# Placing the first head's keys before its queries, spreading the top-k search, and subtracting low parts by accumulating DMAs

## The chip, the cores and the metric

The kernel runs on one core of a Trainium2 chip. The metric is device time in microseconds (us) of one execution. The engines are TensorE (PE for matmuls, PEld for its weight loads), VectorE (DVE), ScalarE (ACT), GpSimd (POOL) and SyncE (SP), whose queue issues most of the DMAs.

## The reference

One decoder layer on 512 tokens of width 1024: a half-step SwiGLU FFN, a mixer with two attention branches, and a second half-step FFN.

```python
x = x + 0.5 * swiglu_ffn(x, ffn1_norm, ...)
h = rms_norm(x, mix_norm)
(fq, fk, fv, ff, dq, dk, dv, iq, ik, iw, ga, gb) = split_columns(h @ w_in)
# branch A, 8 heads: forgetting attention
o_a = softmax(norm(fq) @ norm(fk).T * scale + cum[t] - cum[s], causal) @ fv     # cum = cumsum(log_sigmoid(ff + b))
# branch B, 8 heads with one shared key and value: only the 128 best keys of each query
score = sum_h iw[t, h] * relu(iq[t, h] . ik[s])
o_b = softmax(norm(dq) @ norm(dk).T * scale + bias[t - s], on top_k(score, 128)) @ dv
merged = sigmoid(ga) * (o_a @ w_branch_a) + sigmoid(gb) * (o_b @ w_branch_b)
x = x + merged @ w_out
x = x + 0.5 * swiglu_ffn(x, ffn2_norm, ...)
```

(The two softmax lines are shortened here; the reference works in blocks of 128 queries.)

## The kernel before

Every fp32 operand is split into a high part in TensorE's fast format and a low part, the rest, and a product is three matmuls (lines 130 to 132): high by high, low by high, high by low. For a weight, SP loads a chunk of 128 x 1024 into one of three raw buffers (`ra`, `rb`, `rc`), ACT casts it to the high part `wh` (line 124), and `lo_eng` subtracts to make the low part `wl` (line 125). `wh` and `wl` have three buffers each, so the cast of a chunk waits until TensorE has left the chunk three places earlier. In the mixer `lo_eng` is GpSimd until head 2 and VectorE after that.

The mixer's projections are "units", kept in one list: w_s (small columns), four units of indexer queries, then the 256-column units fk0, fq0, fv0, fk1, fq1, fv1, dq0, dq1 (keys, queries and values of four forgetting heads each, then queries of the sparse branch), then gates and branch products. A 256-column unit has two chunks of 48 matmuls each. `prod.run(us, upto)` issues TensorE work from this list for so many microseconds by a fixed table price (0.64 for six matmuls of 256 columns), not beyond unit `upto`. TensorE's order is written out by hand; the other engines' order comes from a scheduler, and each engine works strictly in its order.

When fk0 or fq0 is done, `normed` (ACT `kn` L627, ACT `sqh` L519, DVE `ss` L521 and L522, POOL `rh` L524, POOL `kn` L630) normalizes it. `get_k` and `get_q` transpose one head pair on TensorE (`ps_k`, `ps_q`, L530), split the result on ACT (`hi`) and DVE (`lo`, L514) and `place` the halves by DMAs on SP's queue (four for queries, eight for keys).

After the indexer products (`ps_ix`) comes a prelude to the 16 heads: TensorE works on fk0, fq0 and fv0 while VectorE runs the top-k search, 16 rounds of `max` and `match_replace` (L767, L769) over three score tiles, 99 steps in all. In that prelude also stand the keys of the sparse branch (`dsa_keys`: DVE scales `sd` by `rh`, L722, TensorE transposes it to `ps_dk`) and the forget gate's cumulative sum (`forget`: matmuls `pc`, DVE `cum`, transposes `ps_ct`). Then each head g has four steps s: weigh the head before (`pt` transposes, `po` products), one softmax block (`ps_qk`, DVE L817, ACT L819, POOL L821), and `prod.run(FILL[g], limit)`, which fills TensorE's time. `limit` is unit 13 (the last 256-column unit) for heads below 6, the four early gates up to head 9 step 1, and everything after.

The prelude before the change:

```python
while prod.at < 7:                      # through fk0 and fq0
    prod.run(MM); topk_run(TOPK_PRE)    # TOPK_PRE = 2 search steps
for g in later: next(g, 0)              # dsa_keys, forget: ps_dk, pc
for step in range(14):
    prod.run(MM, 8); topk_run(TOPK_PRE) # fv0
    # step 5: ps_ct, step 7: get_q(0), step 10: get_k(0), step 12: bias
prod.finish(8)
```

In the second half of the heads the bias of the mask (`b`) is made on POOL for every softmax block (L893 and L894, later L897).

Of the kernel before, what the change touches and what calls it, by code (L numbers as in the profile page):

```python
# [11 lines left out]
F32 = mybir.dt.float32  # L12
F32R = mybir.dt.float32r
AF = mybir.ActivationFunctionType
OP = mybir.AluOpType
# [3 lines left out]
P = 128  # L19
# [8 lines left out]
FILL = (2.1, 2.3, 2.0, 2.0, 1.7, 1.7, 1.7, 1.7, 2.0, 2.0, 1.4, 1.5, 1.2, 1.2, 1.9, 2.3)  # L28
FILL_LAST = 0.8
FILL_IX = 0.5  # L30
TOPK_PRE, TOPK_BEAT = 2, 1
EARLY_GATES = 4
MM = 0.64
WARM = 9
# [3 lines left out]
EPS = 1e-6  # L38
BIG = 1e30
S_W = 208  # L40
GA = ("g_ffn1", "g_mix", "g_ffn2")


# [7 lines left out]
def tile_hybrid_layer(ctx: ExitStack, tc: tile.TileContext, a: dict):  # L51
# [48 lines left out]
    lo_eng = [V]  # L100
# [5 lines left out]
    def raw_tile(tag):  # L106
        return wpool.tile([P, 1024], F32, tag=tag, bufs=1, name=tag)

    def split_w(raw, f=1024):
        wh = wpool.tile([P, 1024], F32R, tag="wh", name="wh")  # L110
        wl = wpool.tile([P, 1024], F32R, tag="wl", name="wl")
        S.copy(wh[:, :f], raw[:, :f])  # L112
        V.tensor_sub(wl[:, :f], raw[:, :f], wh[:, :f].bitcast(F32))  # L113
        return wh, wl

    def load_w(src, n, m, raw=None):
        f = n * m
        if raw is None:
            raw = raw_tile(next(raw_tags))
        wh = wpool.tile([P, 1024], F32R, tag="wh", name="wh")  # L120
        wl = wpool.tile([P, 1024], F32R, tag="wl", name="wl")
        with tc.high_priority(offset=1 if first else 30):
            nc.sync.dma_start(raw[:, :f].rearrange("p (n m) -> p n m", n=n), src)
            S.copy(wh[:, :f], raw[:, :f])
            lo_eng[0].tensor_sub(wl[:, :f], raw[:, :f], wh[:, :f].bitcast(F32))
        return (wh[:, :f].rearrange("p (n m) -> p n m", n=n),
                wl[:, :f].rearrange("p (n m) -> p n m", n=n))

# [365 lines left out]
    with tc.tile_pool(name="mix", bufs=1) as mp, ExitStack() as att_ctx:  # L494
# [79 lines left out]
        def tm_proj(ws, cols, done):  # L574

            def run():
                ps = [acc_tile("ps_t")[:, :2 * cols].rearrange("p (u c) -> p u c", u=2) for _ in range(2)]
                for c in range(2):
                    wh, wl = ws[c]()
                    for t in range(NT):  # L580
                        for kk in range(4):
                            k = 4 * c + kk
                            mm3(ps[t // 2][:, t % 2], xh[k][:, t * P:(t + 1) * P], xl[k][:, t * P:(t + 1) * P],
                                wh[:, kk], wl[:, kk], k == 0 and t % 2 == 0, k == KD - 1 and t % 2 == 1)
                            if (c, t, kk) != (1, 3, 3):
                                yield MM / 2
                done(ps)
                yield MM / 2
            return run

        chunks = []

        def weight(src, n, m):

            me = len(chunks)
            chunks.append([src, n, m, None])

            def take():
                for c in chunks[me:me + 3]:
                    if c[3] is None:  # L600
                        c[3] = load_w(*c[:3])
                return chunks[me][3]
            return take

        def small_done(ps):
# [53 lines left out]
            gb.append(g)  # L659

        def tm256(name, n, done):
            return tm_proj([weight(a[name][n][:, 4 * c:4 * c + 4], 4, 256) for c in range(2)], 256, done)

        oA = ([mp.tile([P, T], F32R, tag=f"oh{c}", name="oAh") for c in range(4)],
              [mp.tile([P, T], F32R, tag=f"ol{c}", name="oAl") for c in range(4)])
        units = [tm_proj([weight(a["w_s"][:, 4 * c:4 * c + 4], 4, S_W) for c in range(2)], S_W, small_done)]
        units += [fm_proj(weight(a["w_iq"][c], KD, P), (xh, xl), KD, iq_done) for c in range(4)]
        units += [tm256("w_fk", 0, normed("fk0")), tm256("w_fq", 0, normed("fq0")), tm256("w_fv", 0, values(0)),
                  tm256("w_fk", 1, normed("fk1")), tm256("w_fq", 1, normed("fq1")), tm256("w_fv", 1, values(1)),
# [109 lines left out]
        def topk_run(n):  # L779

            nonlocal topk_debt
            topk_debt += n
            with tc.issue_after(anchor[0].ins) if anchor[0] else nullcontext():
                while topk_debt >= 1:
                    next(topk, 0)
                    topk_debt -= 1
# [71 lines left out]
        def get_q(g):  # L858

            nm, c = ("fq", g // 2) if g < H else ("dq", g // 2 - 4)  # L860
            prod.finish({"fq0": 7, "fq1": 10, "dq0": 12, "dq1": 13}[f"{nm}{c // 2}"])
            gain = gq[:, 0:1] if g < H else gq[:, 1:2]
            parts = halves(columns(tn[f"{nm}{c // 2}"], c % 2, "ps_q"), gain)
            out = [at.tile([P, T], F32R, tag=tag, bufs=2, name="st") for tag in ("qh", "ql")]
            for hf, st in enumerate(out):
                place(st, hf, parts[0], hf)
                place(st, 1 - hf, parts[1], hf)
            return out
# [29 lines left out]
                return b[:, :n]  # L898
            return bias

        while prod.at < 7:
            prod.run(MM)
            topk_run(TOPK_PRE)
        for g in later:
            next(g, 0)
        for step in range(14):
            prod.run(MM, 8)
            topk_run(TOPK_PRE)
            if step == 5:
                next(later[1], 0)  # L910
            if step == 7:
                nq = get_q(0)
            if step == 10:
                nk = get_k(0)
            if step == 12:
                nb = get_bias(0)
        prod.finish(8)


        probs = {}  # L920
        flipped = None
# [172 lines left out]
```

## Time and profile before

| | |
|---|---|
| three runs, us | 1115.91, 1113.08, 3799.8 |
| median, us | 1115.91 |
| span of the profiled execution, us | 1111.9 |
| instructions | 17413 |
| busy in the span | PE 98%, PEld 87%, DVE 69%, ACT 49%, POOL 20% |

No device time stands beside the profiled execution's span; the two close runs are 1.2 and 4.0 us above it. A profile row gives the start, the duration, the engine, the line, the operation and its tiles; in square brackets stands how long the engine sat idle before it and what ended that. TensorE's matmuls overlap, so the spacing of their starts, not their duration, tells what one costs.

### The profile page before, as it was taken

The page shows a single profiled execution, that of the slowest core. Times are in us where ns is not written, and L with a number is a line of the kernel's source. Part 1 is how long each engine was busy: PE and PEld are TensorE (multiplying, and loading weights), DVE is VectorE, ACT ScalarE, POOL GpSimd, SP SyncE. Part 2 cuts the span into 40 slices and gives each one's busy share as a digit, 9 for nine tenths or more (in the row PEclk, how much of TensorE's full clock was granted, in tenths as well). Part 3 has the DMA queues.
Part 4 walks back from the last instruction along what each step waited for, and adds up shares of the span by engine and source line. Part 5 has one row for each costly group of instructions (what it writes and reads, how often), then busy time and mean ns, then how long its engine had stood idle before and what let it go on. Part 6 is the DMA issues. An engine that isn't in the chain of part 4 may idle for free.

```text
span 1111.9 us, 17413 instructions
## 1 busy us (share of the span) xinstructions
PE 1084.2 (98%) x6664; PEld 967.0 (87%) x6664; DVE 769.8 (69%) x1228; ACT 539.5 (49%) x862; POOL 218.5 (20%) x263
## 2 busy tenths in 40 slices
PE   8999999999999997899999999999999999999998
PEld 6788899989988897899778778888889899989997
DVE  5995578746966599966664666764976478755963
ACT  5653155513644653467655676443544245522551
POOL 0000000000002347677842561000000000000000
PEclk9999999999999999899999999999999999999999
DMA  7334235532442224335324411433245325432441
GB/s 244 107 98 146 88 97 151 139 100 84 110 115 92 76 76 118 110 112 151 101 76 143 122 59 38 126 121 97 93 124 143 94 77 153 135 97 91 124 115 67
DMA packets 43236, 122.61 MB, mean 110 GB/s; under 512 B 5641, under 2 KB 6025, under 8 KB 43153
## 3 DMA queue, kind: packets, MB, share of 16 engines
q1 hardware_dynamic: 38976, 113.89, 33.7%
q0 software_dynamic: 4032, 7.34, 3.9%
q8 instruction: 53, 0.87, 0.3%
q10 hardware_dynamic: 144, 0.26, 0.1%
q14 instruction: 31, 0.25, 0.1%
HBM read 103.63 MB, written 2.11 MB: 95 GB/s over the span
## 4 chain that ended last, share of the span: by engine, by line
PE 81%; DVE 8%; ACT 4%; POOL 3%; issue 3%; DMA 2%; SPq 0%; POOLq 0%; DVEq 0%; ACTq 0%
PE pd L131 7%; PE pd L132 7%; PE pd L130 7%; PE pB L132 4%; PE pB L131 4%; PE pB L130 4%; PE pC L132 3%; PE pA L132 3%; PE pA L131 3%; PE pC L131 3%; PE pA L130 3%; PE pC L130 3%; PE ps_f L130 2%; PE ps_f L131 2%; PE ps_f L132 2%
## 5 line engine op out<-in xcount | busy, mean ns | idle before, releaser
L131 PE MATMUL pd<-al,wh 128*128 128x512 f32 (+1 forms) x294 | 113.4, 386 | 0.5 <-DVE al L207 0.5
L130 PE MATMUL pd<-ah,wh 128*128 128x512 f32 (+1 forms) x294 | 113.4, 386 | 0.2
L132 PE MATMUL pd<-ah,wl 128*128 128x512 f32 (+1 forms) x294 | 113.1, 385 | 0.0
L205 POOL DMA_DIRECT2D al<-gu x20 | 17.1, 855 | 428.9 <-ACT al L204 428.9
L112 ACT CAST wh<-s 128x1024 fp32r<-128x1024 f32 x48 | 50.6, 1055 | 93.9 <-PE pB L131 39.3
L406 DVE SCALAR_TENSOR_TENSOR x<-pd,x 128x512 f32<-128x512 f32 (+1 forms) x49 | 33.3, 680 | 88.6 <-PE pd L132 88.4
L130 PE MATMUL ps_t<-wh,xh 128*128 128x256 f32 (+1 forms) x288 | 83.2, 289 | 0.0
L131 PE MATMUL ps_t<-wl,xh 128*128 128x256 f32 (+1 forms) x288 | 82.7, 287 | 0.0
L132 PE MATMUL ps_t<-wh,xl 128*128 128x256 f32 (+1 forms) x288 | 82.6, 287 | 0.0
L130 PE MATMUL pB<-tbh,wh 128*128 128x256 f32 x256 | 71.4, 279 | 0.0
L131 PE MATMUL pB<-tbl,wh 128*128 128x256 f32 x256 | 71.4, 279 | 0.0
L132 PE MATMUL pB<-tbh,wl 128*128 128x256 f32 x256 | 71.4, 279 | 0.0
L130 PEld LDWEIGHTS pd<-ah,wh 128*128 128x128 f32 x294 | 55.2, 188 | 11.9 <-ACT ah L202 1.0
L131 PEld LDWEIGHTS pd<-al,wh 128*128 128x128 f32 x294 | 55.2, 188 | 11.8 <-DVE al L207 1.1
L132 PEld LDWEIGHTS pd<-ah,wl 128*128 128x128 f32 x294 | 55.2, 188 | 11.0
L113 DVE TENSOR_TENSOR wl<-s,wh 128x1024 fp32r<-128x1024 f32 x48 | 58.5, 1219 | 3.8 <-ACT wh L112 3.8
L131 PEld LDWEIGHTS ps_t<-wl,xh 128*128 128x128 f32 x288 | 56.7, 197 | 0.5
L130 PEld LDWEIGHTS ps_t<-wh,xh 128*128 128x128 f32 x288 | 56.8, 197 | 0.4
L132 PEld LDWEIGHTS ps_t<-wh,xl 128*128 128x128 f32 x288 | 56.7, 197 | 0.0
L112 ACT CAST wh<-re 128x1024 fp32r<-128x1024 f32 (+1 forms) x27 | 27.8, 1028 | 57.4 <-PE pd L131 22.2
L112 ACT CAST wh<-ra 128x1024 fp32r<-128x1024 f32 (+1 forms) x29 | 29.8, 1029 | 51.6 <-PE pd L131 23.4
L819 ACT ACTIVATE p<-p,mn 128x512 f32<-128x512 f32 (+1 forms) x64 | 35.9, 561 | 37.0 <-DVE mn L817 36.8
(326 smaller groups left out, 3604.9 us busy)
## 6 DMA issues: line engine op xcount, KB each, us to landing
rc<-in_w_pair_dram SPq DMA_DIRECT2D x13, 512.0 KB, 3.6
re<-in_w_pair_dram SPq DMA_DIRECT2D x13, 512.0 KB, 3.6
ra<-in_w_pair_dram SPq DMA_DIRECT2D x13, 512.0 KB, 3.5
rd<-in_w_pair_dram SPq DMA_DIRECT2D x13, 512.0 KB, 3.6
rb<-in_w_pair_dram SPq DMA_DIRECT2D x12, 512.0 KB, 3.7
al<-gu POOLq DMA_DIRECT2D x20, 256.0 KB, 4.1
ra<-in_w_down_dram SPq DMA_DIRECT2D x7, 512.0 KB, 3.5
rc<-in_w_down_dram SPq DMA_DIRECT2D x7, 512.0 KB, 3.6
```

The lines of the kernel that those rows point to most:

```text
L112: S.copy(wh[:, :f], raw[:, :f])
L113: V.tensor_sub(wl[:, :f], raw[:, :f], wh[:, :f].bitcast(F32))
L130: PE.matmul(out, lh, rh, start=start, stop=False, **more)
L131: PE.matmul(out, lh, rl, start=False, stop=False, **more)
L132: PE.matmul(out, ll, rh, start=False, stop=stop, **more)
L205: G.dma_start(l, u, accum_op=OP.add)
L406: V.scalar_tensor_tensor(x[d][:, cols], ps, 0.5, x[d][:, cols], op0=OP.mult, op1=OP.add)
L819: S.activation(p, p, AF.Exp, bias=mn, scale=-1.0, accum_out=rs)
```

## The change

The prelude is now counted in table time: 53 steps of 0.64, until 33.5 is reached, with one search step each instead of two, up to unit 9, so that most of fk1 is done there too. At table times, "milestones" issue the rest: at 2.0 the sparse keys and the cumulative sum, at 7.0 the transposes of the sum, at 16.6 the keys of head 0, at 27.6 its queries, at 28.6 its bias. The chunks of all 256-column units get their low part from ACT (`wl = -wh`) and a DMA on GpSimd's queue that adds the raw chunk to it. The tiles `wh` and `wl` grow from 1024 to 1088 columns, and the chunks of the 256-column units and of w_s lie 8 columns (32 bytes) into theirs.

```diff
-TOPK_PRE, TOPK_BEAT = 2, 1
+TOPK_PRE, TOPK_BEAT = 1, 1
+PRELUDE = 33.5
+W_COLS, W_AT = 1088, 8
...
-    def load_w(src, n, m, raw=None):
+    def load_w(src, n, m, raw=None, at=0):
...
-        wh = wpool.tile([P, 1024], F32R, tag="wh", name="wh")
-        wl = wpool.tile([P, 1024], F32R, tag="wl", name="wl")
+        wh, wl = (wpool.tile([P, W_COLS], F32R, tag=nm, name=nm)[:, at:at + 1024] for nm in ("wh", "wl"))
         with tc.high_priority(offset=1 if first else 30):
             nc.sync.dma_start(raw[:, :f].rearrange("p (n m) -> p n m", n=n), src)
             S.copy(wh[:, :f], raw[:, :f])
-            lo_eng[0].tensor_sub(wl[:, :f], raw[:, :f], wh[:, :f].bitcast(F32))
+            if lo_eng[0] is None:
+                S.mul(wl[:, :f], wh[:, :f].bitcast(F32), -1.0)
+                G.dma_start(wl[:, :f], raw[:, :f], accum_op=OP.add)
+            else:
+                lo_eng[0].tensor_sub(wl[:, :f], raw[:, :f], wh[:, :f].bitcast(F32))
...
         def tm256(name, n, done):
-            return tm_proj([weight(a[name][n][:, 4 * c:4 * c + 4], 4, 256) for c in range(2)], 256, done)
+            return tm_proj([weight(a[name][n][:, 4 * c:4 * c + 4], 4, 256, W_AT, True) for c in range(2)], 256, done)
...
-        units = [tm_proj([weight(a["w_s"][:, 4 * c:4 * c + 4], 4, S_W) for c in range(2)], S_W, small_done)]
+        units = [tm_proj([weight(a["w_s"][:, 4 * c:4 * c + 4], 4, S_W, W_AT) for c in range(2)], S_W, small_done)]
...
-        while prod.at < 7:
-            prod.run(MM)
+        ahead = {}
+        milestones = [(2.0, lambda: [next(g, 0) for g in later]),
+                      (7.0, lambda: next(later[1], 0)),
+                      (16.6, lambda: ahead.update(k=get_k(0))),
+                      (27.6, lambda: ahead.update(q=get_q(0))),
+                      (28.6, lambda: ahead.update(b=get_bias(0)))]
+        spent = 0.0
+        while spent < PRELUDE:
+            prod.run(MM, 9)
+            spent += MM
             topk_run(TOPK_PRE)
-        for g in later:
-            next(g, 0)
-        for step in range(14):
-            prod.run(MM, 8)
-            topk_run(TOPK_PRE)
-            if step == 5:
-                next(later[1], 0)
-            if step == 7:
-                nq = get_q(0)
-            if step == 10:
-                nk = get_k(0)
-            if step == 12:
-                nb = get_bias(0)
-        prod.finish(8)
+            while milestones and milestones[0][0] <= spent:
+                milestones.pop(0)[1]()
+        nq, nk, nb = ahead["q"], ahead["k"], ahead["b"]
```

`weight` passes `at` and `by_dma` on to `load_w` and sets `lo_eng[0]` to None for the chunks that go by DMA. Three places show how this moves instructions.

TensorE at the transposes of the sparse keys, before (`wl_4088` is fq0's second chunk; 156 matmuls of 256 columns stand between the last indexer product and the transposes):

```order
L131 MATMUL ps_t_4264<-wl_4088,xh_3169 128x256
L132 MATMUL ps_t_4264<-wh_4087,xl_3170 128x256
L530 MATMUL ps_dk_4281<-ident_87,sd_3387 128x128 x4
L752 MATMUL pc_4288<-lf_3973,trin_92 128x8
L752 MATMUL pc_4288<-lf_3973,ones_75 128x8
```

The same place now (`wl_3759` is fk0's second chunk; 24 matmuls stand between):

```order
L135 MATMUL ps_t_3830<-wl_3759,xh_3290 128x256
L136 MATMUL ps_t_3830<-wh_3758,xl_3291 128x256
L534 MATMUL ps_dk_4015<-ident_87,sd_3387 128x128 x4
L758 MATMUL pc_4022<-lf_3976,trin_92 128x8
L758 MATMUL pc_4022<-lf_3976,ones_75 128x8
```

The transposes have moved ahead of 132 matmuls. VectorE's list from the last score mask (`sc3`, L805, now L811) to the fourth scale of `sd` holds the same instructions as before, but for one reduce of fk0 (`ss`, L521) that now stands later.

GpSimd after the scales' factors, before (`wl_4088` is fv0's first chunk here, `wl_4166` its second; `kn_4059` and `kn_4070` are the halves of fk0):

```order
L524 TENSOR_TENSOR rh_3952<-ss_3949,nhalf_100 128x1
L125 TENSOR_TENSOR wl_4088<-rb_4086,wh_4087 128x1024
L524 TENSOR_TENSOR rh_4067<-ss_4064,nhalf_100 128x8
L630 TENSOR_TENSOR kn_4059<-kn_4059,rh_4067 128x512
L524 TENSOR_TENSOR rh_4078<-ss_4075,nhalf_100 128x8
L125 TENSOR_TENSOR wl_4166<-rc_4164,wh_4165 128x1024
L630 TENSOR_TENSOR kn_4070<-kn_4070,rh_4078 128x512
```

And now (`wl_4099` and `wl_4174` are fv0's chunks, `kn_4071` and `kn_4082` fk0's halves):

```order
L528 TENSOR_TENSOR rh_3955<-ss_3952,nhalf_100 128x1
L528 TENSOR_TENSOR rh_4079<-ss_4076,nhalf_100 128x8
L636 TENSOR_TENSOR kn_4071<-kn_4071,rh_4079 128x512
L127 DMA wl_4099<-rb_4097 128x1024
L528 TENSOR_TENSOR rh_4090<-ss_4087,nhalf_100 128x8
L127 DMA wl_4174<-rc_4172 128x1024
L636 TENSOR_TENSOR kn_4082<-kn_4082,rh_4090 128x512
```

The DMA for fv0's first chunk now stands behind the whole normalization of fk0's first half, and that half's mean (`ss_4076`, L526) stands on VectorE behind 29 search instructions after the score mask, where 10 stood before.

TensorE in head 5 from step 2's weighing to step 3, before:

```order
L838 MATMUL po<-ph,fv 128x384
L839 MATMUL po<-pl,fv 128x384
L557 MATMUL ps_qk<-kh,st 128x128
L558 MATMUL ps_qk<-kl,st 128x128
L130 MATMUL ps_t<-wh,xh 128x256
L131 MATMUL ps_t<-wl,xh 128x256
L132 MATMUL ps_t<-wh,xl 128x256
```

And now:

```order
L844 MATMUL po<-ph,fv 128x384
L845 MATMUL po<-pl,fv 128x384
L561 MATMUL ps_qk<-kh,st 128x128
L562 MATMUL ps_qk<-kl,st 128x128
L834 MATMUL pt<-ident,p 128x128
L844 MATMUL po<-ph,fv 128x256
L845 MATMUL po<-pl,fv 128x256
```

Step 3 of head 5 has lost its 15 fill matmuls, and step 2 has three of 512 columns where 18 of 256 stood. The same happens in head 8 step 3 (three of nine are left) and head 9 steps 0 and 1 (none of nine, none of six): 69 matmuls of 256 columns that the prelude now holds are missing from the heads.

More of the change, by code (lines that the diff above doesn't have):

```diff
@@ L107, in raw_tile, with split_w @@
         return wpool.tile([P, 1024], F32, tag=tag, bufs=1, name=tag)
-    def split_w(raw, f=1024):
-        wh = wpool.tile([P, 1024], F32R, tag="wh", name="wh")
-        wl = wpool.tile([P, 1024], F32R, tag="wl", name="wl")
+    def split_w(raw, f=1024, at=0):
+        wh, wl = (wpool.tile([P, W_COLS], F32R, tag=nm, name=nm)[:, at:at + 1024] for nm in ("wh", "wl"))
         S.copy(wh[:, :f], raw[:, :f])
@@ L119, in load_w @@
             raw = raw_tile(next(raw_tags))
-        wh = wpool.tile([P, 1024], F32R, tag="wh", name="wh")
-        wl = wpool.tile([P, 1024], F32R, tag="wl", name="wl")
+        wh, wl = (wpool.tile([P, W_COLS], F32R, tag=nm, name=nm)[:, at:at + 1024] for nm in ("wh", "wl"))
         with tc.high_priority(offset=1 if first else 30):
@@ L591, in tile_hybrid_layer, with weight @@
         chunks = []
-        def weight(src, n, m):
+        def weight(src, n, m, at=0, by_dma=False):
             me = len(chunks)
-            chunks.append([src, n, m, None])
+            chunks.append([src, n, m, at, by_dma, None])
             def take():
                 for c in chunks[me:me + 3]:
-                    if c[3] is None:
-                        c[3] = load_w(*c[:3])
-                return chunks[me][3]
+                    if c[5] is None:
+                        by, lo_eng[0] = lo_eng[0], None if c[4] else lo_eng[0]
+                        c[5] = load_w(*c[:3], at=c[3])
+                        lo_eng[0] = by
+                return chunks[me][5]
             return take
```

## The prediction

> **What bounds the kernel now.** I read the page first, then windows over the middle of the kernel, then TensorE's waits there, then the engines' instructions in order of time.
>
> ```profile
> span 1111.9 us, 17413 instructions
> PE 1084.2 (98%) x6664; PEld 967.0 (87%) x6664; DVE 769.8 (69%) x1228; ACT 539.5 (49%) x862; POOL 218.5 (20%) x263
> 420.00:450.00 30.00, 21.66 (x162) 20.40 (x162) 28.08 (x82) 10.79 (x17) 21.23 (x20) 0.91 0.54 150
> 450.00:480.00 30.00, 26.92 (x191) 26.00 (x190) 28.28 (x85) 12.72 (x30) 19.49 (x22) 0.86 0.35 98
> 480.00:510.00 30.00, 29.26 (x230) 28.40 (x231) 19.82 (x53) 20.40 (x48) 21.34 (x31) 1.00 0.46 121
> 510.00:540.00 30.00, 28.06 (x216) 26.36 (x213) 17.81 (x48) 21.12 (x48) 23.67 (x36) 1.00 0.49 136
> ```
>
> A window shows its length and then the busy time of PE, PEld, DVE, ACT and POOL, and the granted clock. TensorE sets the end: of 27.7 us idle (1111.9 less 1084.2), 11.4 lie between 420 and 480, the only place where the clock falls too. That is all the change can win. VectorE is full there: 28 of 30. What TensorE waits for:
>
> ```profile
> PE ps_qk L557 <- DMA kh<-hi: 3.8, 1, 3.8
> PE ps_q L530 <- POOL kn L630: 2.0, 1, 2.0
> PE ps_ct L758 <- DVE cum L753: 1.6, 1, 1.6
> PE pt L828 <- DVE lo L514: 1.5, 1, 1.5
> PE ps_k L530 <- DVE pl L833: 1.3, 1, 1.3
> PE ps_qk L558 <- DMA kl<-lo: 0.9, 1, 0.9
> 447.39 0.41 PE L131 MATMUL ps_t<-wl,xh 128*128 128x256 f32 x1
> 447.61 0.41 PE L132 MATMUL ps_t<-wh,xl 128*128 128x256 f32 x1
> 452.02 0.28 PE L131 MATMUL ps_t<-wl,xh 128*128 128x256 f32 x1
> 452.14 0.28 PE L132 MATMUL ps_t<-wh,xl 128*128 128x256 f32 x1
> ```
>
> Four waits belong to the prelude and head 0's first product: 3.8 + 2.0 + 1.6 + 0.9 = 8.3. Two fall in head 1: 2.8. After each group matmuls start every 0.22 us instead of every 0.12. Some 18 fill matmuls and three products ran slow each time: 18 x 0.10 + 0.4 = 2.2. Together 8.3 + 2.2 + 2.8 + 2.2 = 15.5 us, the ceiling of the gain.
>
> **Keys first.** Keys are transposed 108 + 54 = 162 matmuls before the first product of head 0, 19 us at 0.12, where 27 (3.2 us) stood. Their eight DMAs land well inside that: 3.8 and 0.9 go. So does the 2.0, as fq0 is finished some 90 matmuls ahead of its transposes. Next late are the queries: 54 matmuls, 6.5 us, for ACT's and VectorE's halves, SP's issues and the landing.
>
> ```profile
> 437.49 0.73 DVE L514 SCALAR_TENSOR_TENSOR lo<-ps_q,gq,hi 128x512 fp32r<-128x512 f32 x1
> 435.38 0.69 ACT L513 ACTIVATE hi<-ps_q,gq 128x512 fp32r<-128x512 f32 x1 [2.33 <-PE ps_q L530]
> 438.46 1.10 SPq L552 DMA_DIRECT2D st<-lo  x2
> st<-lo SPq DMA_DIRECT2D x16, 128.0 KB, 3.8
> ```
>
> 0.4 (transposes) + 0.69 + 0.73 + 1.1 + 3.8 = 6.7. I take a wait of 0.5, bounds 0 and 2 (SP may first stand before a weight load, which now waits for the adding DMA to release its raw buffer).
>
> **The sparse keys sooner.** The transposes `ps_dk` now follow the last indexer product after 24 matmuls. TensorE is in order, so everything behind waits for the fourth scale of `sd`.
>
> ```profile
> 402.91 0.39 PE L558 MATMUL ps_ix<-ikl,st 128*128 128x512 f32 x1
> 421.85 0.60 PE L530 MATMUL ps_dk<-ident,sd 128*128 128x128 f32 x4
> 402.56 0.29 DVE L805 TENSOR_TENSOR sc<-sc,cpos 128x128 f32<-128x128 f32 x1
> 405.86 2.23 DVE L805 TENSOR_TENSOR sc<-sc,cpos 128x128 f32<-128x128 f32 x1
> 411.21 2.26 DVE L722 TENSOR_SCALAR sd<-sd,rh 128x128 f32<-128x128 f32 x1
> 413.92 0.67 DVE L521 TENSOR_REDUCE ss<-sqh 128x8 f32<-128x512 f32 x1
> 415.83 0.26 DVE L722 TENSOR_SCALAR sd<-sd,rh 128x128 f32<-128x128 f32 x1
> 405.53 2.40 POOL L125 TENSOR_TENSOR wl<-ra,wh 128x1024 fp32r<-128x1024 f32 x1 [6.38 <-ACT wh L124]
> ```
>
> TensorE arrives at 403.14 + 24 x 0.12 = 406.0. VectorE's list from 405.86 to the fourth scale is the same but for one reduce; it ended at 416.1. Two of its instructions took 2.0 us more than their like (0.29, 0.26) while GpSimd ran a subtraction of 2.40; these subtractions go. 416.1 - 2.0 - 2.0 - 0.6 = 411.5. So a wait of 5.5 us arises where the transposes came at 421.85 with none, and it is longer than the waits after which the clock fell: 2.2 more. I take 7.7; bounds 4 (VectorE somewhat early, clock kept) and 9.7 (the two conflicts stay). The 1.6 before `ps_ct` goes: VectorE has `cum` by about 417, TensorE needs it after 42 more matmuls.
>
> **Low parts by DMA.** Sixteen chunks. ACT gains a negation each, GpSimd gives up 2.4 us and takes an issue:
>
> ```profile
> L204 ACT ACTIVATE al<-ah x28: 625/633/637, 48.3 to 1060.0; 128x512 fp32r<-128x512 f32 x28
> L205 POOL DMA_DIRECT2D al<-gu x20: 841/858/862, 161.9 to 1061.0; - x20
> DMA to landing us min/median/max: 3.3/4.1/6.4
> q0 software_dynamic: 4032, 7.34, 3.9%
> 416.78 1.65 POOL L524 TENSOR_TENSOR rh<-ss,nhalf 128x8 f32<-128x8 f32 x1 [3.40 <-DVE ss L522]
> 418.51 1.05 POOL L630 TENSOR_TENSOR kn<-kn,rh 128x512 f32<-128x512 f32 x1
> 421.86 1.47 DVE L767 MAX8 m<-sc 128x8 f32<-128x512 f32 x3
> ```
>
> ACT: 16 x 1.27 (twice 633) = 20 us on an engine busy 11 to 13 of 30, hidden. The FFN's adding DMAs carry 256 KB, 28 of them, 3.9% of 1111.9 = 43.4 us, or 1.55 each; one of 512 KB should land after 4.1 + 1.55 = 5.65 us, bounds 4.1 and 8.2. Whose cover is thinnest? fv0's first chunk. Its DMA stands on GpSimd behind `rh` and `kn` of fk0, whose mean VectorE reaches 19 search instructions after the fourth scale: at 0.49 (1.47 over 3) 9.4 us, with 1.7 for the others, 422.6. Plus 1.65 + 1.05: issue at 425.3, landing at 431. TensorE needs it after the wait (411.5), the transposes and sums (2.6), 126 matmuls (15.1), `ps_ct` 0.4 and the slow clock 2.2: 431.8. Covered by under a microsecond, 2 us late at 8.2. fk0's second half then ends near 433, where `ps_k` arrives at 432.5. I take 1.0 for both.
>
> The Trainium skill (SBUF — State Buffer, section Who interferes with whom) has a rule against such DMAs: GpSimd cannot write a DMA's descriptors while VectorE holds the shared port in a two-port mode. The 28 adding DMAs here issue in 841 to 862 ns among a busy VectorE, which does not show it; by the rule each could be late by one VectorE instruction, and the sum would be 0.7 worse.
>
> In head 1 the 2.8 us and their slow clock came from the same conflict:
>
> ```profile
> 463.35 1.88 DVE L522 TENSOR_SCALAR ss<-ss 128x8 f32<-128x8 f32 x1
> 419.33 0.25 DVE L522 TENSOR_SCALAR ss<-ss 128x8 f32<-128x8 f32 x1
> ```
>
> With the subtractions gone, and a shorter search backlog before it, I let all 5.0 go.
>
> **Search spread.** 53 steps precede head 0 instead of 79. The other 26, 13 us of VectorE, go to heads 2 to 5, where it was busy 18 to 20 of 30. They delay `pl` and the softmax by half a microsecond a step at most, mostly under fill: 1.0, bounds 0 and 4.
>
> **fk1 in the prelude.** Its 69 matmuls (8.3 us) are missing in head 5 steps 2 and 3 and in heads 8 and 9. There TensorE meets waits of other engines sooner.
>
> ```profile
> 532.04 1.76 POOL L894 TENSOR_SCALAR_AFFINE_SELECT b<-b 128x128 f32<-128x128 f32 x3
> 534.25 0.51 PE L557 MATMUL ps_qk<-kh,st 128*128 128x512 f32 x1 [1.73 <-DVE mn L817]
> 577.07 0.50 PE L838 MATMUL po<-ph,dvv 128*128 128x512 f32 x1 [0.81 <-DVE o L851]
> ```
>
> In head 5 VectorE waited for GpSimd's mask at 533.8 already; now dq1's normalization (2 x 2.7 us) comes into that queue, so perhaps 1 us more is lost. At 577 the wait hangs on copies that follow TensorE's own product, which comes some 4 us sooner of 4.8: 1 us lost. Together 2, bounds 0 and 8.3. The Trainium skill (TensorE: Matmul & The Clock Gate, section HAM oscillation) has the clock fall only at idle gaps over about 3.4 us. Here it fell after 1.3 and 1.5 with four transposes between, so I don't count on these holes keeping it; by the rule they would cost no clock, by the rows up to 2.2 each.
>
> The 32 bytes and the wider tiles: no row shows an effect of an address; 0, bounds -1 and +1.
>
> **The sum.** -15.5 + 0.5 + 7.7 + 1.0 + 1.0 + 2.0 = -3.3. Span 1111.9 - 3.3 = 1108.6; the close runs lie 1.2 and 4.0 above the span, so 1109.8 to 1112.6: **1111**.
>
> **Rivals.** First, the holes lose all (slower): head 5 and heads 8 to 9 are bound by GpSimd's and VectorE's chains, not by TensorE, so taking fill away shortens nothing. Price 8.3 + two clock drops 4.4 = 12.7 in place of 2.0: +7.4, about 1122. It decides from 5.3 us (3.3 + 2.0) of loss on. For it: GpSimd's 24 of 30 at 510 to 540 and the waits above; against: those waits were short. Second, fewer conflicts pay everywhere and the holes are free: 1.0 and 2.0 vanish, and the 2.7 us of idle between 480 and 540 too, with a wait at `ps_dk` of 4: 5.7 + 3.7 better, about 1102. For it: VectorE's stretched instructions; against: GpSimd's queue stays. Third, an adding DMA of 512 KB takes 8.2 us or more: 2 to 3 us at fv0, again at the queries, with another clock drop: +5, about 1115, no gain.
>
> **How the numbers follow.** Forecast 0.5 (1107 to 1114), holes 0.18 (1115 to 1124), fewer conflicts 0.17 (1100 to 1106), late DMAs 0.15 (1113 to 1118). The range 1102 to 1119 leaves out about half of the second's and a third of the first's. 2% is 22 us, more than the ceiling of 15.5 and than any rival; about this much is told from no change. Faster 0.01, slower 0.02, within 0.97.
>
> **What would show it.** A wait of TensorE near 5.5 at `ps_dk` for VectorE's `sd`, with slow matmuls behind; no wait over 1 us for `kh` or `kl`; no GpSimd subtraction in fk0 to dq1, and no `ss` near 2 us; adding DMAs landing near 5.7; waits at head 6 step 0 and at head 8's first `po`. If `ps_dk` waits under 3, or the holes together over 5, I am wrong there.

## The result and the profile after

The changed kernel takes 1126.21 us (median of 1124.27 to 1128.26) beside 1114.49 for the kernel before in the same comparison: ratio 1.0114, 95% interval 1.0091 to 1.0138. The median of 1114.49 counts one execution of 3799.8 us, which the ratio leaves out; by the ratio the change is slower by about 12.7 us. That is less than 2%, and it lies outside the range that I gave (1102 to 1119). The profiled execution took 1126.32 us with a span of 1124.6, so the two spans differ by 12.7 as well, and the traces can be set against each other as they stand. The changed kernel's lines are numbered four to six higher than those of before (L534 is the old L530, L823 the old L817).

First the page of the changed kernel, span and busy time of each engine, and then its windows of 30 us (length; PE, PEld, DVE, ACT, POOL busy; granted clock; DMA share; GB/s).

```profile
span 1124.6 us, 17434 instructions
PE 1088.3 (97%) x6664; PEld 969.9 (86%) x6664; DVE 757.1 (67%) x1224; ACT 554.7 (49%) x878; POOL 199.3 (18%) x267
```

```profile
390.00:420.00 30.00, 25.66 (x151) 23.60 (x150) 26.21 (x73) 15.55 (x30) 4.71 (x7) 0.85 0.48 123
420.00:450.00 30.00, 30.00 (x254) 29.92 (x254) 20.41 (x57) 17.34 (x26) 14.86 (x13) 0.98 0.70 158
450.00:480.00 30.00, 22.60 (x170) 21.91 (x168) 12.07 (x39) 15.48 (x29) 16.05 (x25) 0.89 0.72 165
480.00:510.00 30.00, 27.87 (x224) 26.89 (x223) 20.87 (x68) 20.10 (x44) 19.67 (x32) 1.00 0.84 202
510.00:540.00 30.00, 25.97 (x201) 24.25 (x200) 23.86 (x67) 20.66 (x46) 21.03 (x32) 1.00 0.59 153
540.00:570.00 30.00, 25.72 (x122) 21.21 (x121) 18.54 (x50) 17.77 (x41) 20.95 (x33) 0.83 0.37 94
```

TensorE is idle for 36.3 us (1124.6 less 1088.3) where it was 27.7, and busy for 4.1 more on the same 6664 matmuls: that is half clock. The stretch from 420 to 450, the worst of before, is full now. But 4.3 us are lost ahead of it, 7.4 behind it, and 2.1, 4.0 and 4.3 in the heads, with the clock down in three places (0.85, 0.89, 0.83). The waits of TensorE name them (total, times, longest):

```profile
PE ps_qk L561 <- DMA st<-lo: 6.8, 1, 6.8
PE ps_dk L534 <- DVE sd L728: 4.3, 3, 3.5
PE pt L834 <- POOL p L827: 3.4, 4, 2.0
PE ps_qk L561 <- DVE mn L823: 3.0, 2, 1.8
PE pt L834 <- DVE pl L839: 2.5, 2, 2.0
PE po L844 <- DVE o L857: 2.0, 3, 1.4
PE po L845 <- DVE pl L839: 1.9, 4, 0.8
PE ps_qk L561 <- DMA kh<-hi: 1.9, 2, 1.1
```

The old waits for `kh` before head 0, for `kn`, for `cum`, and for `pl` and `lo` in head 1 are all gone. In their place stands one wait of 6.8 for the queries `st` of head 0, 4.3 at `ps_dk`, and a spread of small ones in the heads.

Where the 12.7 us came from is read at two places where TensorE stands at the same product in both kernels: head 0's first product with the low keys (`kl`), and in head 1 the low half of the third weighing product (`po<-pl`). First before, then after:

```profile
446.62 0.77 PE L558 MATMUL ps_qk<-kl,st 128*128 128x512 f32 x1 [0.92 <-DMA kl<-lo]
479.97 0.38 PE L839 MATMUL po<-pl,fv 128*128 128x256 f32 x1 [0.23 <-DVE pl L833]
```

```profile
462.05 0.63 PE L562 MATMUL ps_qk<-kl,st 128*128 128x512 f32 x1
489.15 0.27 PE L845 MATMUL po<-pl,fv 128*128 128x256 f32 x1
```

After is 15.4 later at the first place, of which 8.2 are the 69 matmuls that it has done more by then: it has lost 7.2. At the second it is 9.2 later, so head 0 and head 1 won 6.2 back. At the end it is 12.7 later with the 69 matmuls no longer ahead: what follows lost 12.7 - 9.2 + 8.2 = 11.7, and at head 10's first product it is 12.2 later already, so all but about half a microsecond of this falls in heads 2 to 9. So 7.2 - 6.2 + 11.7 = 12.7. The larger loss lies in the heads, not in the prelude that the change rewrites.

### The profile page after: what moved, and what is told of

It is laid out like the page before. It is cut to its first block, busy times and chain, and to the rows that moved or that the text cites. A ratio compares the mean times of both kernels' runs of the same rounds, so it can differ in the third digit from the quotient of the medians.

```text
span 1124.6 us, 17434 instructions
## 1 busy us (share of the span) xinstructions
PE 1088.3 (97%) x6664; PEld 969.9 (86%) x6664; DVE 757.1 (67%) x1224; ACT 554.7 (49%) x878; POOL 199.3 (18%) x267
## 4 chain that ended last, share of the span: by engine, by line
PE 80%; DVE 6%; DMA 4%; issue 3%; ACT 3%; POOL 3%; SPq 0%; POOLq 0%; ACTq 0%; DVEq 0%
PE pd L135 7%; PE pd L136 7%; PE pd L134 7%; PE pB L134 4%; PE pB L136 4%; PE pB L135 4%; PE pC L136 3%; PE pA L134 3%; PE pC L134 3%; PE pA L136 3%; PE pA L135 3%; PE pC L135 3%; PE ps_f L134 2%; PE ps_f L135 2%; PE ps_f L136 2%
## 5 line engine op out<-in xcount | busy, mean ns | idle before, releaser
L113 ACT CAST wh<-rc 128x1024 fp32r<-128x1024 f32 (+1 forms) x28 | 28.8, 1029 | 49.8 <-PE pd L135 20.1
```

## The experiments

Three theories of mine had to be told apart, each with its rival: that the transposes `ps_dk` come too soon for VectorE (rival: VectorE's list is late as a whole); that the adding DMAs fill the DMA engines when head 0's queries are placed (rivals: the order alone does it, or SP's queue does); that the second unit of keys (fk1), done in the prelude, leaves steps of the heads without fill (rivals: the spread search, or GpSimd's queue). Medians are in us; ratios are to the kernel before on the same chip, whose median in these comparisons was 1112.7 to 1113.5.

**Low parts by GpSimd again.**

```diff
-        return tm_proj([weight(a[name][n][:, 4 * c:4 * c + 4], 4, 256, W_AT, True) for c in range(2)], 256, done)
+        return tm_proj([weight(a[name][n][:, 4 * c:4 * c + 4], 4, 256, W_AT, False) for c in range(2)], 256, done)
```

> The changed kernel, its sixteen low parts subtracted by GpSimd again, all else as changed. Theory (adding DMAs crowd the DMA engines just when head 0's queries are placed): TensorE's wait for st<-lo, 6.8 us, falls below 2 with its slow clock, and the waits for kh and kl in heads 1 and 3 (3.0 together) below 1; GpSimd's 2.4 us subtractions come back and stretch VectorE by some 2 to 4: about 1117 (1114 to 1121). Rival (the order alone does it, weight loads and placements in one stretch of time): the wait stays above 5 and the time at 1124 to 1128.

1125.26, ratio 1.0101 (1.0085 to 1.0118): the time of the changed kernel. (GpSimd makes thirteen of the sixteen; the last three are VectorE's, to which `lo_eng` turns at head 2.) Yet the theory's wait went as it said: no wait for `st` is left, nor any of the waits for `kh`. The placements of `st` land in a third of the time; the changed kernel from 430 to 462 and this run from 430 to 460 (KB each, median us to landing):

```profile
st<-hi SPq DMA_DIRECT2D x2, 128.0 KB, 8.1
st<-lo SPq DMA_DIRECT2D x2, 128.0 KB, 6.9
```

```profile
st<-hi SPq DMA_DIRECT2D x2, 128.0 KB, 2.2
st<-lo SPq DMA_DIRECT2D x2, 128.0 KB, 2.3
```

New waits took their place: 10.6 for `mn` (longest 3.7) and 5.5 instead of 3.5 at the first `ps_dk`, since VectorE's stretched instructions are back. So adding DMAs and GpSimd's subtractions are two ways to lose about the same here, and the time alone would have told me that neither matters.

**The kernel before with adding DMAs alone.**

```diff
-            lo_eng[0].tensor_sub(wl[:, :f], raw[:, :f], wh[:, :f].bitcast(F32))
+            if lo_eng[0] is None:
+                S.mul(wl[:, :f], wh[:, :f].bitcast(F32), -1.0)
+                G.dma_start(wl[:, :f], raw[:, :f], accum_op=OP.add)
+            else:
+                lo_eng[0].tensor_sub(wl[:, :f], raw[:, :f], wh[:, :f].bitcast(F32))
...
-        return tm_proj([weight(a[name][n][:, 4 * c:4 * c + 4], 4, 256) for c in range(2)], 256, done)
+        return tm_proj([weight(a[name][n][:, 4 * c:4 * c + 4], 4, 256, True) for c in range(2)], 256, done)
```

> The kernel before with nothing but its sixteen low parts by negation on ScalarE and adding DMA. Theory (the adding DMAs crowd the others): the wait for kh before head 0's first product grows from 3.8 to 7 or more, waits for kh and kl appear in heads 1 to 3: slower, 1117 to 1122. Rival (the adding DMAs are harmless, and VectorE is freed of GpSimd's subtractions): no wait for kh above 4, the waits for pl and lo in head 1 (2.8) gone: 1109 to 1113.

1116.97, ratio 1.0037 (1.0022 to 1.0052), 4 us slower. The wait before head 0's first product grew from 3.8 to 6.2, and a second one for `kh`, 1.1, appeared at head 4; the waits for `pl` and `lo` in head 1 fell from 2.8 to 1.9. So adding DMAs cost time without the new order too, but not in the prelude: head 0's first product came at 444.8, where it came at 444.9 before, and TensorE only stood longer in front of it, having lost less ahead of it. Heads 0 and 1 won 4.1. The loss follows from head 3 on, 5.4 in head 3 alone, with waits of 1.3 for `kn`, 2.1 for `pl` and 1.1 for `kh` and a clock of 0.92 and 0.91 in the two windows from 500 to 520.

**Sparse keys later.**

```diff
-        milestones = [(2.0, lambda: [next(g, 0) for g in later]),
-                      (7.0, lambda: next(later[1], 0)),
+        milestones = [(9.0, lambda: [next(g, 0) for g in later]),
+                      (14.0, lambda: next(later[1], 0)),
```

> The changed kernel, the transposes of the sparse keys and what follows them put 66 matmuls later (table time 9 instead of 2), the cumulative sum's 14 instead of 7. Theory (TensorE came to the transposes before VectorE's scales): the waits before ps_dk, 4.3, and the half clock behind them, some 1.5 to 2, go: 1120 (1118 to 1122). Rival (VectorE's list is late as a whole, so the wait moves to the cumulative sum, the keys or the queries): 1124 to 1128.

1114.47, ratio 1.0012 (1.0001 to 1.0023): 11.7 below the changed kernel, twice what I expected. Windows of 10 us over the place, of the changed kernel and then of this run:

```profile
400.00:410.00 10.00, 6.75 (x53) 6.38 (x51) 9.71 (x32) 5.30 (x12) 3.17 (x6) 1.00 0.57 132
410.00:420.00 10.00, 8.91 (x40) 8.27 (x41) 9.97 (x32) 2.16 (x4) 0.49 (x1) 0.56 0.29 79
```

```profile
400.00:410.00 10.00, 10.00 (x83) 9.84 (x82) 9.74 (x33) 6.50 (x14) 3.02 (x5) 1.00 0.64 145
410.00:420.00 10.00, 10.00 (x89) 10.00 (x88) 9.97 (x31) 5.63 (x8) 6.30 (x5) 1.00 0.62 149
```

No idle time is left, and the clock stays at 1.00 where it was 0.56. From the first `ps_dk` to the first fill behind the `pc` sums took 6.3 us (410.25 to 416.59) in the changed kernel and 2.6 here; the next 42 fill matmuls took 7.2 there and 5.0 here. Less the 0.8 of waits between the transposes, the half clock cost 3.7 - 0.8 + 2.2 = 5.1 us, more than the wait itself.

**The second unit of keys out of the prelude.**

```diff
-            prod.run(MM, 9)
+            prod.run(MM, 8)
...
-                      (27.6, lambda: ahead.update(q=get_q(0))),
-                      (28.6, lambda: ahead.update(b=get_bias(0)))]
+                      (24.0, lambda: ahead.update(q=get_q(0))),
+                      (25.0, lambda: ahead.update(b=get_bias(0)))]
```

> The changed kernel with the second unit of keys kept out of the prelude, so that its 69 matmuls fill heads 5, 8 and 9 again as before; queries and bias at table times 24 and 25 so that some 60 matmuls still stand between the queries' transposes and head 0. Theory (holes where fill is missing): head 5's waits for pl, lo and mn, 4.3, and the slow clock behind them go, and about 1 at head 8: 1118 to 1121. Rival (the search, spread into heads 2 to 5, delays VectorE): these waits stay, 1124 to 1128.

1120.57, ratio 1.0064 (1.0047 to 1.0082). Head 5's waits for `pl` and `lo` and its slow clock went, as the theory said; and the wait for `st` grew from 6.8 to 12.0, since the unit had been its cover: 21 matmuls stand between the queries' transposes and head 0's first product, 54 in the changed kernel, and I had meant this edit to leave 60. By the same two-place reading the prelude lost 11.4 against the kernel before and the heads won 4.0, where the changed kernel's heads lost 5.5 in all: the unit costs the heads 9.5 us, and spares the prelude 4.2.

**79 search steps before head 0 again.**

```diff
-TOPK_PRE, TOPK_BEAT = 1, 1
+TOPK_PRE, TOPK_BEAT = 1.5, 1
```

> The changed kernel with 1.5 search steps a turn in the prelude, so that 79 steps precede head 0 as before instead of 53. Theory (the steps left over delay VectorE in heads 2 to 5): the waits there for pl and mn, about 3.5 of the 7.9 us of extra idle, shrink: 1122 to 1124. Rival (missing fill alone does it): these waits stay, and the denser search makes the scales of sd and the norms of fk0 and fq0 late: 1126 to 1129.

1124.14, ratio 1.0098 (1.0081 to 1.0115). The interval overlaps that of the changed kernel, so the spread search costs 2 us at most, and that is not certain. Head 5's waits are still there (2.3 for `pl`, 1.3 for `lo`, and 1.2 for `kl` at the start of head 6): the search is not their cause.

**The three losses taken out together.** Later sparse keys, no second unit, low parts by GpSimd: the edits of the first, third and fourth runs, whose main lines are

```diff
-        return tm_proj([weight(a[name][n][:, 4 * c:4 * c + 4], 4, 256, W_AT, True) for c in range(2)], 256, done)
+        return tm_proj([weight(a[name][n][:, 4 * c:4 * c + 4], 4, 256, W_AT, False) for c in range(2)], 256, done)
...
-        milestones = [(2.0, lambda: [next(g, 0) for g in later]),
+        milestones = [(9.0, lambda: [next(g, 0) for g in later]),
...
-            prod.run(MM, 9)
+            prod.run(MM, 8)
```

> The order of the change alone, with the three suspected losses taken out together: sparse keys 66 matmuls later, no second unit of keys in the prelude, low parts by GpSimd. Theory (the losses are these three and add up): no wait at ps_dk, none for st, heads as in the run without that unit but with GpSimd's subtractions: about 7 below the kernel before, 1105 (1102 to 1109). Rival (GpSimd's subtractions or VectorE's list bind as soon as one wait goes): 1110 to 1115.

1105.97, ratio 0.9930 (0.9912 to 0.9947): 7.5 us faster than the kernel before, near the 7 that I expected and about 2 more than the plain sum of the three runs (12.7 less 11.7, 5.6 and 1.0 is a gain of 5.6). What is left of the change was worth having, and its gain had been spent on three companions (the early sparse keys, the second unit and the adding DMAs). By the two places it does not lie where I had put it: the prelude is 1.4 longer than before, heads 0 and 1 are 6.4 shorter and the rest 1.9. The search ends at 521 here and ended at 477 before, within head 1; VectorE is busy 16.6 of the 27.3 us of heads 0 and 1, where it was 30.7 of 33.9. That points to the spread search rather than to the order of keys and queries, but no run takes the two apart. What is left in the prelude is GpSimd: `kn` of fq0 waits behind a subtraction (437.41), and TensorE behind `kn`:

```profile
437.41 2.36 POOL L129 TENSOR_TENSOR wl<-rb,wh 128x1024 fp32r<-128x1024 f32 x1
439.72 1.05 POOL L636 TENSOR_TENSOR kn<-kn,rh 128x512 f32<-128x512 f32 x1
440.82 0.44 PE L534 MATMUL ps_q<-ident,kn 128*128 128x128 f32 x2 [3.20 <-POOL kn L636]
```

**Adding DMAs only for late chunks.** The run before it, with

```diff
-        return tm_proj([weight(a[name][n][:, 4 * c:4 * c + 4], 4, 256, W_AT, False) for c in range(2)], 256, done)
+        return tm_proj([weight(a[name][n][:, 4 * c:4 * c + 4], 4, 256, W_AT, name + str(n) in ("w_fv1", "w_dq0", "w_dq1")) for c in range(2)], 256, done)
```

> As the run before in this list, with adding DMAs for the chunks of fv1, dq0 and dq1 alone, whose loads come after head 0's placements, and GpSimd for the chunks of fk0, fq0, fv0, fk1 and fq1. Theory (adding DMAs cost only where they meet the placements, and in the heads they spare VectorE the stretched instructions): 1101 to 1105, some 3 below the other. Rival (they delay the keys of heads 2 to 5 as well): 1106 to 1111.

1110.70, ratio 0.9967 (0.9953 to 0.9980): 4.7 above the run before it. My theory missed; the rival said 1106 to 1111. Six adding DMAs behind head 0 cost more than they spare; a wait of 2.2 for `kl` in head 3 is new.

**Placements from another queue.** Later sparse keys as in the third run, and head 0's placements issued by ScalarE (S):

```diff
-            nc.sync.dma_start(dst[at_ * DH:at_ * DH + DH].bitcast(F32), src[hf * DH:hf * DH + DH].bitcast(F32))
+            place_q[0].dma_start(dst[at_ * DH:at_ * DH + DH].bitcast(F32), src[hf * DH:hf * DH + DH].bitcast(F32))
...
+        place_q[0] = S
         ahead = {}
...
+        place_q[0] = nc.sync
         nq, nk, nb = ahead["q"], ahead["k"], ahead["b"]
```

> The changed kernel with the sparse keys 66 matmuls later (1114.5 in the run of that alone), and head 0's and 1's twelve placements issued from ScalarE's queue instead of SP's. Theory (on SP they stand behind weight loads, which wait for adding DMAs to release their raw buffers): the wait for st falls from 5.9 to under 2, 1108 to 1110. Rival (the DMA engines are full, so a sooner issue lands no sooner): the wait stays above 4, 1113 to 1117.

1117.70, ratio 1.0033 (1.0019 to 1.0048): 2 to 3 slower than on SP's queue, and the wait for `st` still 4.7. With no weight load in front of them the placements of `st` needed 5.6 and 7.8 us to land, so a place behind SP's weight loads is not what makes the landings long. The run is no clean test of the queue, though: ScalarE's cast of a weight chunk stood 8.1 us behind its own issues for the keys, and TensorE waited 1.8 for `fv`.

**VectorE subtracts.** Edits of the third and fourth runs, and:

```diff
-                        by, lo_eng[0] = lo_eng[0], None if c[4] else lo_eng[0]
+                        by, lo_eng[0] = lo_eng[0], V if c[4] else lo_eng[0]
```

> As the run with late sparse keys, no second unit of keys in the prelude and GpSimd's subtractions (1106.0), but VectorE subtracts the sixteen low parts (1.22 us each). Theory (a subtraction of 2.40 on GpSimd costs VectorE about 2 in one stretched instruction and GpSimd's own chain 2.4, more than the 1.22 it costs when VectorE does it): the wait of 3.2 for kn and those for sd (1.4) shrink by half or more: 1102 to 1105. Rival (VectorE is full in the prelude, so 1.22 more a chunk makes the norms and softmax late): 1106 to 1110.

1103.90, ratio 0.9922 (0.9905 to 0.9939), 8.7 us faster than the kernel before, in which GpSimd still makes twelve of the sixteen. The waits at `ps_dk` (1.4) are gone and that for `kn` fell from 3.2 to 2.2, less than I expected; the wait for `st` is 4.0, where it was 2.8.

**The address alone.**

```diff
-W_COLS, W_AT = 1088, 8
+W_COLS, W_AT = 1024, 0
```

> The changed kernel with its weight chunks at the start of their buffers again (no 32 bytes further, buffers of 1024 columns). Theory (the address costs nothing): 1126 (1125 to 1127). Rival (the address moves where weight loads or adding DMAs meet other traffic): over 2 us away from that, in either direction.

1125.51, ratio 1.0107 (1.0090 to 1.0123): no effect that can be seen.

**The unit priced without adding DMAs.** Later sparse keys and GpSimd's subtractions, the second unit in the prelude.

```diff
-        return tm_proj([weight(a[name][n][:, 4 * c:4 * c + 4], 4, 256, W_AT, True) for c in range(2)], 256, done)
+        return tm_proj([weight(a[name][n][:, 4 * c:4 * c + 4], 4, 256, W_AT, False) for c in range(2)], 256, done)
...
-        milestones = [(2.0, lambda: [next(g, 0) for g in later]),
+        milestones = [(9.0, lambda: [next(g, 0) for g in later]),
```

> The changed kernel with late sparse keys and GpSimd's subtractions, the second unit of keys still in the prelude: against 1106.0 it prices the moved unit alone. Theory (its 69 matmuls are missing in heads 5, 8 and 9, which wait on VectorE and GpSimd and get no shorter): the prelude gains what the wait for kn and st were (up to 6), the heads lose 8 to 10: 1109 to 1113. Rival (with no adding DMAs the heads give back what the prelude took): 1103 to 1107.

1120.10, ratio 1.0058 (1.0041 to 1.0076): 14.1 above the run without the unit, more than the 8.2 of its matmuls. Both sides missed: by the two places the prelude gained 6.6 from the unit, as I had thought, but the heads lost 19.3. The trace shows where: with the unit done 8 us sooner, its chunks' subtractions and its norms reach GpSimd while heads 1, 2 and 4 need their biases `b` from it. At the start of head 1:

```profile
456.38 2.41 POOL L129 TENSOR_TENSOR wl<-rb,wh 128x1024 fp32r<-128x1024 f32 x1
458.73 1.07 POOL L636 TENSOR_TENSOR kn<-kn,rh 128x512 f32<-128x512 f32 x1
459.76 1.54 POOL L899 TENSOR_SCALAR b<-cb,ncum 128x256 f32<-128x256 f32 x3
461.25 1.68 POOL L528 TENSOR_TENSOR rh<-ss,nhalf 128x8 f32<-128x8 f32 x1
462.87 0.57 POOL L900 TENSOR_SCALAR_AFFINE_SELECT b<-b 128x128 f32<-128x128 f32 x2
463.22 0.42 DVE L823 CUSTOM_DVE_ANT_0 p<-ps_qk,b 128x256 f32<-128x256 f32 x1 [4.40 <-POOL b L900]
463.71 0.66 PE L561 MATMUL ps_qk<-kh,st 128*128 128x512 f32 x1 [3.75 <-DVE mn L823]
```

GpSimd works without a pause from 456.4 to 463.4; the bias stands fifth in its row, VectorE waits 4.4 for it, and TensorE 3.75 for VectorE.

**The same with VectorE subtracting.**

```diff
-                        by, lo_eng[0] = lo_eng[0], None if c[4] else lo_eng[0]
+                        by, lo_eng[0] = lo_eng[0], V if c[4] else lo_eng[0]
...
-        milestones = [(2.0, lambda: [next(g, 0) for g in later]),
+        milestones = [(9.0, lambda: [next(g, 0) for g in later]),
```

> The changed kernel with late sparse keys and the sixteen low parts subtracted by VectorE, the second unit of keys in the prelude: against 1103.9 (the same without that unit) it prices the unit with GpSimd's subtractions gone, where 1120.1 stood against 1106.0 with them. Theory (GpSimd's queue of subtractions, norms and masks makes the long waits for mn): the waits of 3.8, 2.4 and 3.1 go, and the unit costs what its missing fill costs, 2 to 6: 1106 to 1110. Rival (missing fill and the sooner norms alone): the waits stay above 2 each, 1114 to 1118.

1110.25, ratio 0.9977 (0.9967 to 0.9987): the unit now costs 6.3 against the run without it, where it cost 14.1 with GpSimd's subtractions. The waits of 3.75 and 2.4 in heads 1 and 2 are gone; one of 3.1 stays in head 4, and so does head 5's row of 2.4, 1.1 and 1.4. The prelude is clean: the wait for `st` is 0.3.

**Fill spread to cover the holes.** The run before it, with

```diff
-FILL = (2.1, 2.3, 2.0, 2.0, 1.7, 1.7, 1.7, 1.7, 2.0, 2.0, 1.4, 1.5, 1.2, 1.2, 1.9, 2.3)
+FILL = (1.8, 2.0, 1.7, 1.7, 1.4, 1.4, 1.7, 1.7, 2.0, 2.0, 1.4, 1.5, 1.2, 1.2, 1.9, 2.3)
```

> The same with the table's fill of heads 0 to 5 lowered by 0.3 a step (24 steps, 7.2 in all, the table price of the moved unit), so that no step of heads 5, 8 and 9 is without fill. Theory (the loss lies in the steps without fill): 3 to 5 below the run before it in this list. Rival (heads 0 to 5 are bound by other engines' chains, and any matmul taken from them is lost): the same or slower, the waits spread over heads 0 to 5.

1105.28, ratio 0.9931 (0.9918 to 0.9944), 5.0 below the run before it: of the 6.3 that the unit cost there, filling the empty steps won 5.0 back. Head 5's row of waits is gone, and others for `p` (2.5, 2.7 and 1.8 in heads 1, 2 and 5) have come.

**The same fill with adding DMAs.** The third run, with

```diff
-FILL = (2.1, 2.3, 2.0, 2.0, 1.7, 1.7, 1.7, 1.7, 2.0, 2.0, 1.4, 1.5, 1.2, 1.2, 1.9, 2.3)
+FILL = (1.8, 2.0, 1.7, 1.7, 1.4, 1.4, 1.7, 1.7, 2.0, 2.0, 1.4, 1.5, 1.2, 1.2, 1.9, 2.3)
```

> The changed kernel with late sparse keys (1114.5 alone) and the same lowered fill, low parts still by adding DMAs. Theory (the holes of heads 5, 8 and 9 cost 4.8 of waits and a slow clock there): 1109 to 1111. Rival (the loss only moves into heads 0 to 4, where placements of keys land late): 1113 to 1117.

1113.17, ratio 0.9997 (0.9986 to 1.0008): 1.3 below 1114.47, and 7.9 above the same kernel with VectorE's subtractions. The wait for `st` stays at 5.1 and one of 3.3 for `kh` comes in head 2: with adding DMAs the loss moves into the next placements, as the rival said.

**How the DMA engines fill.** The clearest pair is the third run and the twelfth, which differ only in who makes the low parts. DMA queues and landings of both from 420 to 455 (packets, MB, share of the 16 engines; KB each, median us to landing), first with adding DMAs:

```profile
q1 hardware_dynamic: 1913, 4.45, 44.8%
q0 software_dynamic: 720, 2.62, 39.7%
...
kh<-hi SPq DMA_DIRECT2D x4, 128.0 KB, 5.5
kl<-lo SPq DMA_DIRECT2D x4, 128.0 KB, 5.9
st<-hi SPq DMA_DIRECT2D x2, 128.0 KB, 8.0
st<-lo SPq DMA_DIRECT2D x2, 128.0 KB, 6.5
```

```profile
q1 hardware_dynamic: 2076, 5.11, 49.5%
...
kh<-hi SPq DMA_DIRECT2D x4, 128.0 KB, 2.6
kl<-lo SPq DMA_DIRECT2D x4, 128.0 KB, 5.5
st<-hi SPq DMA_DIRECT2D x2, 128.0 KB, 2.3
st<-lo SPq DMA_DIRECT2D x2, 128.0 KB, 2.5
```

Five adding DMAs took 39.7% of 35 us, 13.9 us of all sixteen engines, 2.8 each; the rest moved 4.45 MB in 15.7 us, 3.5 us a MB (3.4 in the twelfth run), 1.8 for a weight chunk. With both on one chunk that is 4.6 us, and TensorE uses up a chunk of 48 matmuls in 5.7. Four fifths of the DMA engines go to weights alone, and twelve placements of 128 KB, 1.6 MB, want 5.5 us more within 25. So it comes out at full, which is what the windows show (the changed kernel and the third run around their placements, then the twelfth run around its own):

```profile
435.00:460.00 25.00, 19.71 (x170) 19.50 (x168) 6.25 (x12) 14.19 (x21) 10.74 (x12) 0.98 1.01 235
425.00:450.00 25.00, 19.65 (x167) 19.24 (x165) 14.73 (x42) 13.99 (x20) 10.76 (x12) 0.98 0.94 231
```

```profile
425.00:446.00 21.00, 20.68 (x176) 20.42 (x175) 21.00 (x53) 9.16 (x15) 8.55 (x9) 1.00 0.63 179
```

DMA share 1.01 and 0.94 against 0.63, and waits of 6.8 and 5.9 against 0.3. The placements of `kl`, 5.9 against 5.5, hardly differ; at head 0 TensorE waits for neither.

SP's queue adds to it. In the changed kernel the high halves `hi` of the queries were ready at 450.1, but SP stood 2.2 us for the adding DMA that had to release a raw buffer, and each pair of placements then took it about 2 us to issue:

```profile
451.48 0.33 SPq L123 DMA_DIRECT2D rb<-in_w_fv_dram  x1
451.91 2.13 SPq L556 DMA_DIRECT2D st<-hi  x2
454.14 1.83 SPq L556 DMA_DIRECT2D st<-lo  x2
```

In the first run, without adding DMAs, a pair took 1.1 to 1.2.

## Why the prediction was wrong, point by point

Put on the two places, my terms were +0.9 for the prelude (-8.3, +0.5, +7.7, +1.0), -7.2 for heads 0 and 1 (-2.2, -2.8, -2.2) and +3.0 for the rest (1.0 and 2.0). Measured were +7.2, -6.2 and +11.7. Two steps failed, the queries in the prelude and the holes in the heads.

**What bounds the kernel, and the ceiling.** The waits were read rightly: the four of the prelude and the two of head 1 went with their half clock, and heads 0 and 1 won 6.2. The ceiling of 15.5 no run came near; with the losses undone the kernel was 7.5 below the one before, and 8.7 with VectorE's subtractions besides. In the sixth run, waits of 3.2 for `kn` and 2.8 for `st` had taken the place of the prelude's old ones.

**The sparse keys.** Mechanism and place right, size short. VectorE's fourth scale ended at 412.1 where I had 411.5, the stretched instructions were gone, and the waits summed to 4.3 against 5.5. The slow clock behind them was taken at 2.2, from the two slow stretches of before; it cost 5.1, since the small transposes and sums run in it first and it lasted until about 421. Together 9.4 against 7.7, near my upper bound of 9.7. The third run, which undid it, won 11.7, 2.3 more than these two sizes.

**The queries.** This is the step that failed first: 0.5, bounds 0 and 2; the wait was 6.8, with half clock behind it. I priced the chain from the transposes to the last landing at 6.7, by the landing of 3.8 that the placements had in the kernel before; it took 13.3 (448.1 to 461.4). The transposes, ScalarE and VectorE needed 2.8 of it where I had 1.8; the placement that ended the wait was issued 3.2 behind them where I had 1.1, and landed after 7.3. I had named SP's stand before a weight load and left it inside the bound of 2. The adding DMA's landing I had at 5.65; the sixteen had medians of 5.4 to 5.7 by buffer, but 6.7 to 8.7 from 430 to 462, where they met the placements, and I asked only whether its own chunk comes in time. I never summed what the DMA engines would have to carry in these 25 us, though my own numbers had the time of a 256 KB adding DMA on them, 1.55. That the adding DMAs are the cause is shown by the first run, where with them alone taken out the wait is gone, and by the pair of the third and twelfth (5.9 against 0.3). No run parts the late issues from the long landings.

**fv0's chunk, 1.0.** Not there: no wait stands at `ps_ct` or `ps_k`. Its adding DMA was issued at 426.6 and landed after 5.3, close to the 425.3 and 5.65 that I had. One count was wrong: of the sixteen subtractions that went, twelve were GpSimd's and four VectorE's.

**Search spread, 1.0.** As a cost not refuted and not shown: at most 2 by the fifth run. As a gain for heads 0 and 1 I had it only in half a sentence, and the sixth run points to it.

**The holes, 2.0.** The other step that failed, and the larger one: behind head 1, 11.7 were lost, against 3.0 for all my terms there. Moving the unit cost the heads 9.5 with adding DMAs (fourth run), 19.3 with GpSimd's subtractions and 12.8 with VectorE's; as fill in the prelude it gave 4.2, 6.6 and 6.1 of that back, so that the whole kernel lost 5.6, 14.1 and 6.3 by the medians. I had given the case that the holes lose all its full price, 8.3 and the clock, with a chance of 0.18, because the waits there were short in the trace of before. Short waits under full fill say nothing of what stands under the fill. In head 5 two waits came, 1.96 and 0.55, with half clock behind the first, in a chain that had been hidden; the wait of 1.76 at the start of head 6 had stood there before, with 1.73. The unit's norms came into GpSimd's queue earlier, which no term of mine held. How the 11.7 splits between empty steps, GpSimd's sooner norms and late placements in the changed kernel itself is not settled: filling the steps gave 5.0 with VectorE's subtractions and 1.3 with adding DMAs.

**The rivals.** The first (holes) happened, and of the third (late adding DMAs) the half at the queries; the half at fv0 did not. Each alone I had put at 1122 and 1115. Their surplus of about 11 and 4 on the forecast of 1111 makes 1126, and that this is the measured time is luck, since the terms under it came out otherwise. My range held the third and not the first nor the two together, though nothing in them excludes the other. The second rival (fewer conflicts) was true of the stretched instructions and worth nothing while the DMAs replaced them.

**The 32 bytes.** Zero, as taken.

The Trainium skill's rule against such DMAs (SBUF — State Buffer, section Who interferes with whom) speaks of the shared port; what cost time here was the DMA engines' share, and the issues on GpSimd took 0.84 to 0.92 us in the changed kernel, close to the 0.84 to 0.86 of twenty of the FFN's 28; the other eight, which I had not counted, took up to 1.05. The idle gap of about 3.4 us that the Trainium skill names for a falling clock (TensorE: Matmul & The Clock Gate, section HAM oscillation) was not needed here: the last section has a fall behind 1.96 us.

## What to carry to other kernels

When a change replaces work on an engine by DMAs, sum the DMA engines' time in the window where they meet the transfers that someone waits for, not just the new transfer's own landing; here 4.6 us of every 5.7 went to weights, and the placements paid. Ask too which queue stands behind such a DMA for its buffer. Fill that is moved ahead leaves its place empty: look at what the waits of that place would be without it, and spread the rest of the fill anew. And where several parts of a change are tried at once, undo them one at a time and then together: a gain of 7.5 us was hidden by three companions, and undoing the adding DMAs alone showed nothing in the time.

## What the runs showed that I had not expected

A gap of 1.96 us halved the clock in one place, and a gap of 2.25 us did not in another. Rows of TensorE and the windows around them, first the changed kernel in head 5, then the ninth run in the prelude:

```profile
544.18 0.58 PE L834 MATMUL pt<-ident,p 128*128 128x128 f32 x2 [1.96 <-DVE pl L839]
544.42 0.67 PE L844 MATMUL po<-ph,fv 128*128 128x384 f32 x1
...
540.00:550.00 10.00, 5.72 (x27) 4.43 (x26) 7.96 (x21) 6.41 (x16) 8.63 (x10) 0.72 0.52 129
```

```profile
436.23 0.33 PE L534 MATMUL ps_q<-ident,kn 128*128 128x128 f32 x1 [2.25 <-POOL kn L636]
...
430.00:440.00 10.00, 6.87 (x58) 6.43 (x56) 10.00 (x29) 3.88 (x6) 7.68 (x11) 1.00 0.75 208
```

After 2.25 us amid dense fill the clock stayed at 1.00. After 1.96 us, with few matmuls around it, the first product already ran slow (0.67 us, where the same takes 0.42 at 559.83), and the clock was 0.72 over the ten. The busy share of the microseconds around the gap may be what matters, but no run here isolates that.

A GpSimd subtraction of 2.4 us cost more than VectorE's own of 1.22: with the unit in the prelude, moving GpSimd's thirteen to VectorE saved 9.9 us (1120.10 against 1110.25), though VectorE was then busy all the 30 us from 420 to 450; without the unit the two stand 2.1 apart, which is within their intervals.
